# First feed-forward product by one level of Strassen's scheme: seven half-size products in place of eight, the norm factor applied behind the second product

## The chip, the core and the metric

One NeuronCore of a Trainium2 chip. Its engines run their own instruction streams and meet through semaphores: PE (TensorE, matrix products into PSUM), DVE (VectorE) and ACT (ScalarE) for work on tiles, POOL (GpSimd), and SP (SyncE), whose queue issues nearly all transfers from memory here. The metric is device time of one execution in microseconds (us); lower is better. Three runs of the kernel before took 1042.26, 1042.49 and 1043.43 us, median 1042.49.

## What is computed

One layer of a streaming encoder for 512 prompt tokens and 64 sample tokens, which the kernel treats as one stream of T = 576 columns, model width D = 1024. The change touches the last step of the layer:

```
h = h + mem_attn(rmsnorm(h), mem_k, mem_v, w_mem_q, w_mem_o)
hn = rmsnorm(h, ln_ffn)
h = h + square(relu(hn @ w_ff1)) @ w_ff2        # 1024 -> 4096 -> 1024
y = rmsnorm(h, ln_final)
```

All inputs are float32. The kernel gets near float32 accuracy from faster products on a rounded type ("fp32r"): each operand is split into a high part (a cast) and a low part (operand minus high part), and a product is the sum of high x high, high x low and low x high, the low x low term being dropped.

## The kernel before

Activations lie transposed: 128 of the 1024 features on the partitions, eight such blocks, the 576 tokens along the free dimension. `hT` holds h in that form. `project` (L168) computes one output block of 128 features for all tokens: for each of two token ranges (256 and 320 columns, `HALVES`) it takes a PSUM bank from the "pr" group (three banks) and goes over the blocks of the contraction, three partial products for each. In the range of 256 columns the two products with the high part of the weights share one matmul of 512 columns (`high_parts`, L184); in the range of 320 they are two matmuls. A function `evac` given by the caller empties the bank.

`weights` and `split_weights` (L154) bring weights: SP loads a raw tile (three buffers), ACT casts it to the high part at L160, and DVE subtracts at L161 to get the low part.

The stages around the change, in the program's order:

1. Output projection of the memory attention: eight `project` calls with `w_mem_o`, whose `add_residual` (L1085) adds the result to `hT`, multiplies it by the gain `ln_ffn`, splits it into `fx`, and adds up the squares for the norm.
2. `norm_columns` (L1112): five small matmuls sum the squares over partitions, POOL takes the power -1/2 (`rpow`), and `row_broadcast` spreads the factor 1/rms over all partitions into `rB`.
3. `ff1(g)` (L1218), for eight groups of four output blocks: `project` over all eight blocks of the contraction; the evacuation multiplies by `rB` (L1226), squares the positive part (L1227), and splits the result into high and low parts (L200, L201).
4. Second product: group g-1 of the hidden features is the contraction (four blocks) for each of eight output blocks; `add_residual` adds each result to `hT` (L1090, L1092). The loop issues `ff1(g)` ahead of the second product of group g-1.
5. The last group's weights for the second product are kept (`last_weights`, L1238), and the last products run in two token ranges (`last_block`, L1247), so that the final norm and the output of the first range overlap the second.

The tiles come from pools: "sp" (small tiles), "wp" (weights), "up" (six large pairs) and "cp" (constants). The order of instructions on each engine is fixed when the program is built, by a planner that follows the dependencies; some parts are kept in written order.

Of the kernel before, what the change touches and what calls it, by code (L numbers as in the profile page):

```python
# [37 lines left out]
def hybrid_layer_kernel(  # L38
# [30 lines left out]
    wp = ctx.enter_context(tc.tile_pool(name="wp", bufs=2))  # L69
    sp = ctx.enter_context(tc.tile_pool(name="sp", bufs=2))  # L70
    tp = ctx.enter_context(tc.tile_pool(name="tp", bufs=2))
    ps = ctx.enter_context(tc.tile_pool(name="ps", bufs=2, space=PSUM))
    dp = ctx.enter_context(tc.tile_pool(name="dp", bufs=1, space=bass.MemoryType.DRAM))
    BANKS = dict(pr=3, ba=2, g0=1, g1=1, gs=1)
# [14 lines left out]
    SHARED = dict(cb="p0", yv="p1", fs="p0", ko="p0", tm="p1", r="on", acc="p1")  # L89
# [12 lines left out]
    def const(shape, name, dt=F32):  # L102
        return cp.tile(shape, dt, tag=name, name=name)

    def mm(out, lhsT, rhs, start=True, stop=True, pin=False):
        i = nc.tensor.matmul(out, lhsT, rhs, start=start, stop=stop)  # L106
        if pin:
            tc.keep_in_program_order(i)

# [54 lines left out]
    def weights(w, c0, kt=KT):  # L164

        return split_weights(w[:, c0 : c0 + P], [P, kt, P])
# [25 lines left out]
    def add_to(dst, b, more):  # L192
        A.copy(dst, more)  # L193
        V.tensor_tensor(dst, b, dst, ALU.add)  # L194
# [886 lines left out]
        nc.sync.dma_start(hT[i], hd[i])  # L1081

    accs = [None]

    def add_residual(m, last, split=None, g0=None, alone=None):  # L1085


        def evac(b, a0, n, more):
            hm = hT[m // 4][:, m % 4, a0 : a0 + n]
            V.tensor_tensor(hm, hm, b, ALU.add)  # L1090
            if more is not None:
                V.tensor_tensor(hm, hm, more, ALU.add)  # L1092
            if not last:
                return
            if split is not None:
                split_to(split, hm, m, a0, gcol[:, g0 + m : g0 + m + 1])
            if m == 0:
                if a0 == 0:
                    accs[0] = small("acc", [P, T])
                A.activation(accs[0][:, a0 : a0 + n], hm, AF.Square)  # L1100
            else:
                sq = small("zr", [P, 320])[:, :n]
# [104 lines left out]
                A.copy(dh, src)  # L1207
# [10 lines left out]
    def ff1(g):  # L1218
        sx = (pair((4, 1, 5)[g % 3], F32R),)
        for i in range(4):  # L1220
            def evac(b, a0, n, more):
                f = small("fs", [P, 320])[:, :n]
                if more is not None:
                    add_to(f, b, more)
                    b = f
                V.tensor_tensor(f, b, rB[:, a0 : a0 + n], ALU.mult)  # L1226
                V.scalar_tensor_tensor(f, f, 0.0, f, ALU.max, ALU.mult)  # L1227
                split_to(sx, f, i, a0)

            project(  # L1230
                weights(w_ff1[0], (4 * g + i) * P), fx, evac, between=broadcast if g == i == 0 else None
            )
        return sx


    wlast = []

    def last_weights(m):  # L1238
        if m == 0:
            wlast.extend(pair(i, F32R) for i in (3, 2))  # L1240
        hi, lo = (view(u, m // 4, 16, P)[:, 4 * (m % 4) : 4 * (m % 4) + 4] for u in wlast)
        raw = wp.tile([P, 4, P], F32, tag="raw", name=nm("raw"), bufs=3)
        nc.sync.dma_start(raw, w_ff2[0, (NG - 1) * 512 :, m * P : (m + 1) * P].rearrange("(k p) n -> p k n", p=P))
        A.copy(hi, raw)
        V.tensor_tensor(lo, raw, hi.bitcast(F32), ALU.subtract)
# [44 lines left out]
        rpow(r2[:, c], r[:, c])  # L1290
        return r2

    pend = ff1(0)
    for g in range(1, NG):
        nxt = ff1(g)
        for m in range(KT):
            project(
                weights(w_ff2[0, (g - 1) * 512 : g * 512, :], m * P, 4), pend, add_residual(m, False), kt=4
            )
            if g == NG - 1:  # L1300
                last_weights(m)
        pend = nxt


    for m in range(KT):
        last_block(m, pend, *HALVES[0])
# [50 lines left out]
```

## Time and profile before

| | |
|---|---|
| time, median of 3 runs | 1042.49 us (1042.26 to 1043.43) |
| profiled execution: span from first to last instruction | 1039.2 us |
| mean granted TensorE clock | 0.998 |
| busy share: PE, DVE, ACT, POOL | 98%, 65%, 43%, 6% |
| instructions of the span | 16983 |
| output projection of the memory attention | ends near 615 us |
| the two feed-forward products | about 615 to 1030 us |

The profile gives for its execution the span alone; the runs' times also hold what lies around it. Lines of a timeline give start and length in us, engine, line of the kernel, operation, written tile and read tiles, shapes and count; in square brackets stands the idle time before and what ended it. A group's line gives count, then busy us in total and the mean ns of one instruction, then idle time before the group's instructions. A windows line gives the window, its length, and for PE, weight loads (PEld), DVE, ACT and POOL the busy us and the count, then the granted clock, the share of the DMA engines and GB/s. Matmuls overlap: one starts before the one before it has drained, so the time that a matmul costs is the distance between starts.

### The profile page before, as it was taken

To read this page: it belongs to the slowest core of one execution; us is meant where nothing else is said; L and a number is where in the kernel's file an instruction comes from. 1 tells how busy PE (TensorE), PEld (TensorE's weight loads), DVE (VectorE), ACT (ScalarE), POOL (GpSimd) and SP (SyncE) were. 2 spreads that over 40 slices of the span, in tenths; PEclk is the share of its full clock that TensorE was granted. 3 is DMA by queue.
4 is the path that set the end of the run, shared out by engine and by line. 5 is a ranking of instruction groups with operands and counts; after the bars stand their busy time and mean duration, and the time that the engine had idled before them with its cause. 6 is when DMAs were issued, how large, how long until landed. Compare 5 with 4: busy or idle time off the path is not lost.

```text
span 1039.2 us, 16983 instructions
## 1 busy us (share of the span) xinstructions
PE 1019.3 (98%) x6566; PEld 931.0 (90%) x6566; DVE 680.0 (65%) x1502; ACT 445.6 (43%) x936; POOL 58.3 (6%) x124
## 2 busy tenths in 40 slices
PE   9999999999999999999999999999999999999996
PEld 7989899998888878999987999999999999999996
DVE  6676784776666676665664756666666666666763
ACT  6654664433465665444543433323222222222344
POOL 3431110100001000000000000000000000000000
PEclk9999999999999999999999999999999999999999
DMA  7433410100321445433120222141313132313312
GB/s 214 128 102 83 116 50 26 38 21 22 110 83 47 145 164 188 136 84 121 41 62 21 81 82 72 41 122 51 113 51 112 54 110 61 112 52 112 96 48 92
DMA packets 139748, 89.97 MB, mean 87 GB/s; under 512 B 5570, under 2 KB 130624, under 8 KB 139156
## 3 DMA queue, kind: packets, MB, share of 16 engines
q1 hardware_dynamic: 139300, 88.24, 29.0%
q8 instruction: 52, 0.85, 0.3%
q10 hardware_dynamic: 368, 0.66, 0.2%
q14 instruction: 28, 0.23, 0.1%
HBM read 79.14 MB, written 9.74 MB: 86 GB/s over the span
## 4 chain that ended last, share of the span: by engine, by line
PE 87%; DVE 3%; issue 2%; POOL 2%; ACT 2%; DMA 1%; POOLq 0%; ACTq 0%; DVEq 0%; SPq 0%
PE pr L106 68%; PE g L106 9%; PE gs L106 5%; PE ba L112 2%; PE g L112 2%; DVE wl L161 0%; PE ba L106 0%; POOL tg L207 0%; DVE p L456 0%; DMA out_dram<-S 0%; DMA S<-in_state_gdn_dram 0%; POOL tiny L207 0%; POOL X L603 0%; DVE on L779 0%; ACT L644 0%
## 5 line engine op out<-in xcount | busy, mean ns | idle before, releaser
L106 PE MATMUL pr<-u,wh 128*128 128x320 f32 (+2 forms) x2680 | 691.4, 340 | 2.1 <-DVE p L322 1.0
L106 PEld LDWEIGHTS pr<-u,wh 128*128 128x128 f32 x2680 | 456.6, 188 | 36.5 <-DVE p L322 1.3
L106 PE MATMUL pr<-u,wl 128*128 128x256 f32 (+1 forms) x1776 | 482.4, 299 | 0.0
L106 PEld LDWEIGHTS pr<-u,wl 128*128 128x128 f32 x1776 | 327.0, 189 | 7.7 <-issue 0.7
L160 ACT CAST wh<-raw 128x1024 fp32r<-128x1024 f32 (+1 forms) x153 | 136.6, 892 | 223.5 <-PE pr L106 214.9
L161 DVE TENSOR_TENSOR wl<-raw,wh 128x1024 fp32r<-128x1024 f32 (+1 forms) x153 | 157.4, 1029 | 52.9 <-ACT wh L160 50.8
L1090 DVE TENSOR_TENSOR u<-u,pr 128x256 f32<-128x256 f32 (+1 forms) x160 | 72.4, 453 | 61.7 <-PE pr L106 59.1
L200 ACT CAST u<-p 128x256 fp32r<-128x256 f32 x64 | 27.8, 434 | 51.8 <-DVE p L1227 51.8
L207 POOL TENSOR_TENSOR tiny<-tiny,nhalf 128x1 f32<-128x1 f32 (+4 forms) x11 | 10.4, 946 | 645.0 <-DVE tiny L1289 409.0
L106 PE MATMUL pr<-wh,u 128*128 128x512 f32 x128 | 41.2, 400 | 0.0
L201 DVE TENSOR_TENSOR u<-p,u 128x256 fp32r<-128x256 f32 x64 | 29.2, 457 | 15.1 <-ACT u L200 15.1
L193 ACT COPY p<-pr 128x256 f32<-128x256 f32 (+1 forms) x42 | 15.6, 372 | 49.4 <-PE pr L106 49.4
L1092 DVE TENSOR_TENSOR u<-u,pr 128x256 f32<-128x256 f32 x80 | 33.6, 420 | 2.4
L194 DVE TENSOR_TENSOR p<-pr,p 128x256 f32<-128x256 f32 (+1 forms) x42 | 17.8, 423 | 25.8 <-ACT p L193 25.7
L456 DVE SCALAR_TENSOR_TENSOR p<-p,gcol,p 128x579 f32<-128x579 f32 x33 | 27.1, 822 | 9.0 <-ACT p L454 8.5
L1226 DVE TENSOR_TENSOR p<-pr,rB 128x320 f32<-128x320 f32 x32 | 15.7, 492 | 25.6 <-PE pr L106 25.6
L1227 DVE SCALAR_TENSOR_TENSOR p<-p 128x256 f32<-128x256 f32 x64 | 29.3, 458 | 2.2
L203 ACT ACTIVATE u<-u,gcol 128x256 fp32r<-128x256 f32 (+1 forms) x32 | 17.0, 533 | 30.4 <-DVE u L1092 30.4
L106 PE MATMUL g<-u,qz 128*128 128x256 f32 (+4 forms) x96 | 29.2, 408 | 0.0
L741 ACT COPY X<-g 128x512 f32<-128x512 f32 (+1 forms) x24 | 13.2, 551 | 34.3 <-PE g L112 34.3
L106 PEld LDWEIGHTS pr<-wh,u 128*128 128x128 f32 x128 | 23.3, 188 | 4.4
L106 PE MATMUL pr<-u,u 128*128 128x320 f32 (+2 forms) x160 | 26.5, 323 | 0.0
(373 smaller groups left out, 1248.9 us busy)
## 6 DMA issues: line engine op xcount, KB each, us to landing
raw<-in_w_ff_dram SPq DMA_DIRECT2D x32, 512.0 KB
raw<-in_w_ff_dram SPq DMA_DIRECT2D x64, 256.0 KB
raw<-in_w_in_dram SPq DMA_DIRECT2D x28, 512.0 KB
raw<-in_w_mem_k_dram SPq DMA_DIRECT2D x8, 512.0 KB
raw<-in_w_mem_v_dram SPq DMA_DIRECT2D x8, 512.0 KB
raw<-in_w_out_dram SPq DMA_DIRECT2D x8, 512.0 KB
raw<-in_w_mem_q_dram SPq DMA_DIRECT2D x8, 512.0 KB
raw<-in_w_mem_o_dram SPq DMA_DIRECT2D x8, 512.0 KB
```

Of the source, the lines that this page charges most:

```text
L106: i = nc.tensor.matmul(out, lhsT, rhs, start=start, stop=stop)
L112: i = nc.tensor.transpose(out, in_, ident[:n, :n])
L160: A.copy(wh, raw)
L161: V.tensor_tensor(wl, raw, wh.bitcast(F32), ALU.subtract)
L194: V.tensor_tensor(dst, b, dst, ALU.add)
L200: A.copy(h, src)
L201: V.tensor_tensor(lo, src, h.bitcast(F32), ALU.subtract)
L203: A.activation(h, src, AF.Identity, scale=g)
L456: V.scalar_tensor_tensor(yv[:, :n], cb[:, i : i + n], cwt[:, m, i : i + 1], yv[:, :n], ALU.mult, ALU.add)
L1090: V.tensor_tensor(hm, hm, b, ALU.add)
L1092: V.tensor_tensor(hm, hm, more, ALU.add)
L1227: V.scalar_tensor_tensor(f, f, 0.0, f, ALU.max, ALU.mult)
```

## The change

The normalised input is no longer formed. The first product runs on h times the gain, without the factor 1/rms. As relu(c x)^2 = c^2 relu(x)^2 for positive c, the squared factor (a reciprocal on DVE, no root) is multiplied onto the second product's sum, behind the product; only the last group of hidden features gets it ahead of the second product.

`combine(m)` forms, while the output projection runs (in the order m = 0, 4, 1, 5, 2, 6, 3, 7), the combinations of the input's four quarters (upper and lower half of the features, first and second 288 tokens) that the scheme needs, and splits them. `ff1_pair(p)` computes two output blocks: it loads a raw tile of 512 x 256 for each half of the features, forms four sums of weight blocks on DVE, splits seven weight blocks, and runs seven products of 4 x 3 matmuls with 288 columns, accumulating in the banks "g0", "gs", "g1" and "ba"; ACT copies intermediate sums out (`keep`), DVE adds them, squares and splits (`put`). The pools "sp" and "wp" are closed ahead of this, and a new pool "fp" takes tiles in the same memory, waiting tile by tile for the old ones. The second product sums over groups in its own buffer `accu`, which is multiplied by the factor and added to `hT` after group 6. The sum of squares moves into a tile of its own ("accq").

```
@@ output projection, first product @@
-    fx = [pair(i, F32R) for i in (3, 2)]
-    for m in range(KT):
-        project(weights(w_mem_o[0], m * P), mo, add_residual(m, True, fx, G_FF))
-    cols, rB = norm_columns(), const([P, T], "rB")
-    broadcast = lambda: row_broadcast(cols, rB, pin=True)
+    NH = T // 2
+    N0, N1 = slice(0, NH), slice(NH, T)
+    B2 = pair(1, F32R)
+    T12, T34 = ([u[:, j].rearrange("p k (i t) -> p i k t", i=2) for j in range(2)] for u in (pair(2, F32R), pair(3, F32R)))
+    B1 = [cp.tile([P, 2, T], F32R, tag=f"qz{i}", name=nm("B1")).rearrange("p j (k t) -> p j k t", k=2) for i in range(2)]
+    def combine(m):
+        scaled[m] = x = small("kd" if m < 4 else "aT", [P, T])
+        A.activation(x, hT[m // 4][:, m % 4, :], AF.Identity, scale=gcol[:, G_FF + m : G_FF + m + 1])
+        k = m % 4
+        if m < 4:
+            hi, lo = (B1[k // 2][:, j, k % 2, :] for j in range(2))
+            A.copy(hi, x[:, N0])
+            V.tensor_tensor(lo, x[:, N0], hi.bitcast(F32), ALU.subtract)
+            return
+        top = scaled[k]
+        t12, t34 = small("p0", [P, 2, NH]), small("an", [P, 2, NH])
+        V.tensor_tensor(t12[:, 0], top[:, N1], top[:, N0], ALU.subtract)
+        V.tensor_tensor(t34[:, 0], x[:, N1], top[:, N1], ALU.subtract)
+        V.tensor_tensor(t12[:, 1], x[:, N1], t12[:, 0], ALU.subtract)
+        V.tensor_tensor(t34[:, 1], x[:, N0], t12[:, 1], ALU.subtract)
+        for (hi, lo), src in (
+            ((T12[j][:, :, k, :] for j in range(2)), t12),
+            ((B2[:, j, k, :] for j in range(2)), x),
+            ((T34[j][:, :, k, :] for j in range(2)), t34),
+        ):
+            A.copy(hi, src)
+            V.tensor_tensor(lo, src, hi.bitcast(F32), ALU.subtract)
+    for m in (0, 4, 1, 5, 2, 6, 3, 7):
+        project(weights(w_mem_o[0], m * P), mo, add_residual(m, True))
+        combine(m)
...
+    V.tensor_scalar(cols, b[:, :5], 1.0 / D, EPS, ALU.mult, ALU.add)
+    V.reciprocal(squared, cols)
+    work.close()
+    fp = ctx.enter_context(tc.tile_pool(name="fp", bufs=1, reuse_waits="tile"))
+    def split(src, tag, bufs, dma=False):
...
+        with tc.high_priority():
+            A.copy(wh, src)
+            V.tensor_tensor(wl, src, wh.bitcast(F32), ALU.subtract)
+    def weights2(w, c0):
+        raw = ft("r2", [P, 4, P], 3)
+        nc.sync.dma_start(raw, w[:, c0 : c0 + P].rearrange("(k p) n -> p k n", p=P))
+        return split(raw, "w2", 3)
+    def ff1_pair(p, sx):
+        raw = []
+        for i in range(2):
+            raw.append(ft("r1", [P, 4, 2 * P], 2))
...
+        A11, A21 = raw[0][:, :, :P], raw[0][:, :, P:]
+        A12, A22 = raw[1][:, :, :P], raw[1][:, :, P:]
+        s12, s34 = (ft(tag, [P, 2, 4, P], 1) for tag in ("s12", "s34"))
+            V.tensor_tensor(s12[:, 0], A21, A22, ALU.add)
+            V.tensor_tensor(s12[:, 1], s12[:, 0], A11, ALU.subtract)
+        a11, ws12 = split(A11, "a1", 1), split(s12, "w12", 1)
+            V.tensor_tensor(s34[:, 1], A12, s12[:, 1], ALU.subtract)
+            V.tensor_tensor(s34[:, 0], A11, A21, ALU.subtract)
+        a2, ws34 = split(raw[1], "a2", 1), split(s34, "w34", 1)
...
+        def put(i, n, b, more):
+            c = ft("c", [P, NH], 3)
+            V.tensor_tensor(c, b, more, ALU.add)
+            V.scalar_tensor_tensor(c, c, 0.0, c, ALU.max, ALU.mult)
+            if p >= 2 * (NG - 1):
+                V.tensor_tensor(c, c, rB[:, n], ALU.mult)
+            hi, lo = (sx[:, j, 2 * (p % 2) + i, n] for j in range(2))
+            A.copy(hi, c)
+            V.tensor_tensor(lo, c, hi.bitcast(F32), ALU.subtract)
+        x, y, z, w = bank("g0"), bank("gs"), bank("g1"), bank("ba")
+        product(1, x, True)
+        s1 = keep(x)
+        product(5, z, True)
+        s5 = keep(z)
+        product(2, y, True)
+        put(0, N0, y[:, :NH], s1)
+        product(6, x, False)
+        s2 = keep(x)
+        product(3, z, False)
+        put(0, N1, z[:, :NH], s2)
+        product(7, x, False)
+        s3 = keep(x)
+        put(1, N1, s3, s5)
+        product(4, w, True)
+        put(1, N0, w[:, :NH], s3)
@@ the loop over groups @@
-    pend = ff1(0)
+    pend = pair(5, F32R)
+    ff1_pair(0, pend)
+    ff1_pair(1, pend)
+    row_broadcast(squared, rB)
     for g in range(1, NG):
-        nxt = ff1(g)
+        nxt = (f1 if g == 1 else odd()) if g % 2 else pair(5, F32R)
         for m in range(KT):
-            project(
-                weights(w_ff2[0, (g - 1) * 512 : g * 512, :], m * P, 4), pend, add_residual(m, False), kt=4
-            )
+            if m % 4 == 0:
+                ff1_pair(2 * g + m // 4, nxt)
+            project(weights2(w_ff2[0, (g - 1) * 512 : g * 512, :], m * P), (pend,), add_group(g - 1, m), kt=4)
             if g == NG - 1:
-                last_weights(m)
+                am, hm = accu[0][m // 4][:, m % 4, :], hT[m // 4][:, m % 4, :]
+                V.tensor_tensor(am, am, rB, ALU.mult)
+                V.tensor_tensor(hm, hm, am, ALU.add)
+                if m >= 4:
+                    last_weights(2 * m - 8)
+                    last_weights(2 * m - 7)
```

In the built program PE's seven products of a pair stand in the order 1, 5, 2, 6, 3, 7, 4; pairs 0, 1 and 2 follow each other with nothing of the second product between them; from pair 5 on product 1 and most of product 5 are moved between the blocks of the second product.

More of the change, by code (lines that the diff above doesn't have):

```diff
@@ L103, in const, with mm @@
         return cp.tile(shape, dt, tag=name, name=name)
-    def mm(out, lhsT, rhs, start=True, stop=True, pin=False):
-        i = nc.tensor.matmul(out, lhsT, rhs, start=start, stop=stop)
+    def mm(out, lhsT, rhs, start=True, stop=True, pin=False, skip_group_check=False):
+        i = nc.tensor.matmul(out, lhsT, rhs, start=start, stop=stop, skip_group_check=skip_group_check)
         if pin:
@@ L1083, in hybrid_layer_kernel @@
     accs = [None]
+    temps = lambda n: small("zr", [P, 320])[:, :n]
     def add_residual(m, last, split=None, g0=None, alone=None):
@@ new lines, in hybrid_layer_kernel @@
+    for m in (0, 4, 1, 5, 2, 6, 3, 7):
+        project(weights(w_mem_o[0], m * P), mo, add_residual(m, True))
+        combine(m)
+    b = bank()
+    for t, (q0, n) in enumerate(QT):
+        mm(b[:, t : t + 1], accs[0][:, q0 : q0 + n], ones[:, 0:1])
+    cols, squared = tiny([P, 5]), tiny([P, 5])
+    V.tensor_scalar(cols, b[:, :5], 1.0 / D, EPS, ALU.mult, ALU.add)
+    V.reciprocal(squared, cols)
+    work.close()
+    fp = ctx.enter_context(tc.tile_pool(name="fp", bufs=1, reuse_waits="tile"))
@@ new lines, in ft @@
+    def ft(tag, shape, bufs, dt=F32):
+        return fp.tile(shape, dt, tag=tag, name=nm(tag), bufs=bufs)
+    temps = lambda n: ft("tm", [P, 320], 2)[:, :n]
+    odd = lambda: ft("f1", [P, 2, 4, T], 1, F32R)
+    f1 = odd()
+    rB = ft("rB", [P, T], 1)
+    def split(src, tag, bufs, dma=False):
+        shape = list(src.shape)
+        wh, wl = (ft(tag + x, shape, bufs, F32R) for x in "hl")
+        with tc.high_priority():
+            A.copy(wh, src)
+            V.tensor_tensor(wl, src, wh.bitcast(F32), ALU.subtract)
+        return wh, wl
@@ L1236, in hybrid_layer_kernel, with add_group, evac @@
+    accu = [None]
+    def add_group(g, m):
+        def evac(b, a0, n, more):
+            am = accu[0][m // 4][:, m % 4, a0 : a0 + n]
+            if g == 0:
+                if more is not None:
+                    add_to(am, b, more)
+                else:
+                    A.copy(am, b)
+                return
+            V.tensor_tensor(am, am, b, ALU.add)
+            if more is not None:
+                V.tensor_tensor(am, am, more, ALU.add)
+        return evac
     wlast = []
```

61 lines of the change are left out of this document (41 added, 20 removed).

## The prediction

> **What bounds the kernel now.** I read the page's first part, then the windows over the feed-forward stages, then the chain of waits.
>
> ```profile
> PE 1019.3 (98%) x6566; PEld 931.0 (90%) x6566; DVE 680.0 (65%) x1502; ACT 445.6 (43%) x936; POOL 58.3 (6%) x124
> ```
> ```profile
> 760.00:820.00 60.00, 60.00 (x380) 56.49 (x380) 39.03 (x77) 16.45 (x30) 0.00 (x0) 1.00 0.28 80
> 880.00:940.00 60.00, 60.00 (x380) 56.56 (x379) 39.02 (x76) 15.83 (x27) 0.00 (x0) 1.00 0.29 83
> ```
> ```profile
> PE 87%; DVE 3%; issue 2%; POOL 2%; ACT 2%; DMA 1%; POOLq 0%; ACTq 0%; DVEq 0%; SPq 0%
> ```
>
> TensorE (PE) never pauses in the two products: 60.00 of 60.00 us in both windows, granted clock 1.00, and the chain is 87% PE. VectorE (DVE) is busy 39.0 of 60. So a matmul less is worth its start-to-start time, as long as DVE keeps pace. The rhythm stands in PE's timeline:
>
> ```profile
> 701.65 0.40 PE L106 MATMUL pr<-u,wh 128*128 128x512 f32 x1
> 701.89 0.28 PE L106 MATMUL pr<-u,wl 128*128 128x256 f32 x1
> 702.01 0.40 PE L106 MATMUL pr<-u,wh 128*128 128x512 f32 x1
> ...
> 703.07 0.40 PE L106 MATMUL pr<-u,wh 128*128 128x512 f32 x1
> ...
> 704.42 0.31 PE L106 MATMUL pr<-u,wl 128*128 128x320 f32 x1
> ...
> 705.30 0.31 PE L106 MATMUL pr<-u,wl 128*128 128x320 f32 x1
> ```
>
> Four 512+256 pairs take 1.42 us (701.65 to 703.07), so 0.355 a pair, of which the 256 takes 0.12 (701.89 to 702.01). Six of 320 columns take 0.88, so 0.147 each.
>
> **The saving on PE.** An output block of the first product now costs 8 x 0.355 + 24 x 0.147 = 6.36 us, the 32 blocks 203.5. Afterwards a pair of blocks is seven products of 12 matmuls, 84 of 288 columns. No row has 288; halfway between 0.120 and 0.147 lies 0.134, which I take, and the ends are 0.120 and 0.147. Sixteen pairs are 1,344 matmuls, 180.1 us. The saving is **23.4 us** (5.9 to 42 by the ends; the 320 rate costs all but a quarter). The second product keeps its matmuls: 1.42 us for a block's 256 columns, 12 x 0.147 = 1.76 for its 320, 12.7 for four blocks.
>
> **What DVE and ACT get instead.** Durations by form:
>
> ```profile
> L161 DVE TENSOR_TENSOR wl<-raw,wh 128x1024 fp32r<-128x1024 f32 x43 | 52.7, 1225 | 13.5 <-ACT wh L160 11.9
> L160 ACT CAST wh<-raw 128x1024 fp32r<-128x1024 f32 x43 | 45.2, 1050 | 63.2 <-PE pr L106 59.6 <-ACT u L1207 2.1 <-issue 1.4
> L161 DVE TENSOR_TENSOR wl<-raw,wh 128x512 fp32r<-128x512 f32 x56 | 38.6, 690 | 7.0 <-ACT wh L160 6.8
> L1090 DVE TENSOR_TENSOR u<-u,pr 128x320 f32<-128x320 f32 x72 | 35.1, 487 | 46.2 <-PE pr L106 45.7
> L160 ACT CAST wh<-raw 128x512 fp32r<-128x512 f32 x56 | 34.7, 620 | 109.5 <-PE pr L106 106.5 <-DMA raw<-in_w_ff_dram 3.0
> L1092 DVE TENSOR_TENSOR u<-u,pr 128x256 f32<-128x256 f32 x72 | 30.2, 420 | 2.2
> L200 ACT CAST u<-p 128x320 fp32r<-128x320 f32 x32 | 14.8, 462 | 7.1 <-DVE p L1227 7.1
> L200 ACT CAST u<-p 128x256 fp32r<-128x256 f32 x32 | 13.0, 406 | 44.7 <-DVE p L1227 44.7
> ```
>
> Between the rows: 288 columns 0.455 on DVE and 0.43 on ACT; 576 columns 0.757 on DVE and 0.68 on ACT. DVE makes for a pair of blocks four sums of weights and one low part of 512 (5 x 0.69), three low parts of 1024 (3.68), and for each of four outputs an add, a square and a low part (12 x 0.455 = 5.46): 12.6 us. With four blocks of the second product (4 x 0.69 of weights, 4 x (0.42+0.42+0.487) of sums, 8.1) a cycle is 20.7 us of DVE against 84 x 0.134 + 12.7 = 24.0 of PE, 86%. On average it fits. Queued instructions also overlap:
>
> ```profile
> 616.82 1.23 DVE L161 TENSOR_TENSOR wl<-raw,wh 128x1024 fp32r<-128x1024 f32 x1 [0.60 <-ACT wh L160]
> 617.96 0.55 DVE L204 SCALAR_TENSOR_TENSOR u<-u,gcol,u 128x320 fp32r<-128x320 f32 x1
> ```
>
> The second starts 1.14 us after the first, 0.09 before its end; I count 0.08.
>
> **Term 1, the entry.** Today the first weights are asked for at 592.68, some 28 us before the factor's root on POOL:
>
> ```profile
> 592.68 19.41 SPq L156 DMA_DIRECT2D raw<-in_w_ff_dram  x4
> ```
> ```profile
> 620.35 1.17 POOL L207 TENSOR_TENSOR tiny<-tiny,nhalf 128x5 f32<-128x5 f32 x1 [144.26 <-DVE tiny L1117]
> 621.57 1.38 PE L106 MATMUL ba<-ident,tiny 128*128 128x128 f32 x10 [0.81 <-POOL tiny L207]
> ```
>
> The entry's one stall is PE's wait for POOL's root, 0.8 to 1.1 us. That root goes. But the new pool "fp" reuses the memory of "sp", and in the built program SP's first weight load waits for DVE's very last subtraction in `combine(7)`, which reads the tile lying under the load's target. Behind it in SP's queue stand all other weight loads. From PE's last matmul of the output projection, DVE has an add and a sum of squares (2 x 0.487), three combinations (3 x 0.455), three low parts (3 x 0.757) and two tiny ones, 5 us, and waits for ACT's square and scaling, 0.46 + 0.68: about 6.1. Then the load:
>
> ```profile
> 605.38 54.40 SPq L156 DMA_DIRECT2D raw<-in_w_ff_dram  x9
> ```
> ```profile
> 608.50:609.00 0.50, 0.50 (x5) 0.50 (x5) 0.00 (x0) 0.00 (x0) 0.00 (x0) 1.00 0.47 129
> 609.00:609.50 0.50, 0.50 (x5) 0.46 (x4) 0.11 (x1) 0.11 (x1) 0.00 (x0) 1.00 0.00 0
> ```
>
> 512 KB asked for at 605.38 into an idle queue stop flowing just before 609.0: 3.6 us. So raw weights at 9.7, the cast 0.62 later, the first matmul near 10.4, where PE has had 2 us of work. From then DVE is the limit: three pairs run back to back, and ahead of the add that frees the first bank of the second product its queue holds 12 instructions of 1024, 25 of 512, 35 of 288 and two small: 14.7 + 17.3 + 15.9 + 0.7 = 48.6 us, 42.8 with all 72 overlaps. That ends at 52.5 to 58.3. Undelayed PE would be there after 252 x 0.134 + three second-product parts (1.42+1.76+1.42) + 1.7 of small matmuls = 40.1. The lag is 12.4 to 18.2; I take 15.0, as some waits for PE break the overlaps, less the 1.1 that goes: **+13.9**.
>
> **Term 2, the clock.** Eight us without a matmul do not occur today except at the end:
>
> ```profile
> 1031.00:1032.00 1.00, 0.36 (x3) 0.12 (x2) 0.16 (x1) 0.00 (x0) 0.75 (x1) 1.00 0.00 0
> ...
> 1034.00:1035.00 1.00, 0.00 (x0) 0.00 (x0) 0.33 (x1) 0.50 (x1) 0.00 (x0) 0.94 1.02 379
> 1035.00:1036.00 1.00, 0.00 (x0) 0.00 (x0) 0.00 (x0) 0.00 (x0) 0.00 (x0) 0.50 1.03 375
> ```
>
> The granted clock is half some 3.5 us after the last matmul, so the first products start at half speed. How long that lasts no row shows; between nothing and the whole first pair (another 11.3 us, part of it under DVE's work) I take **+1**. [...]
>
> **Term 3, the steady cycles.** The order of the program is tight. Between the end of a pair's seventh product and the point where PE needs the first of its three banks back lie product 4 (1.61), blocks of 1.42 + 1.76 + 1.42 and product 1 of the next pair (1.61): 7.82. DVE's list up to the add that frees it (L1374 in the new file) begins behind 0.4 and 1.05 of ACT casts and holds two low parts of 1024, two instructions of 512, five of 288 and two of 256: 1.45 + 2.45 + 1.38 + 2.28 + 0.84 = 8.4, or 7.6 with ten overlaps. That is 0.2 early, or 0.6 late without overlaps. The second bank is needed after 7.82 + 1.76 + 1.42 + 11 x 0.134 = 12.5. Ahead of its add DVE waits for the next pair's raw weights, whose load SP issues only after the low part of "a2", 4.8 us into the list: 4.8 + 3.6 + five of 512 and two of 256 (4.3, overlapped 3.8) = 12.3, again 0.2 early. There are eleven such cycles. I take 0.1 each, **+1** (0 to 11).
>
> **Term 4, the tail.** The norm factor costs two extra 576-wide instructions for each of eight blocks and one of 288 for each of the last eight outputs, and the last weights (eight of 512) now fall into the last four blocks. From the last product to the third bank of the last blocks DVE's list is 10 x 0.69 + 10 x 0.42 + 7 x 0.757 + 4 x 0.487 + 5 x 0.455 = 20.6, or 17.7 overlapped, where PE has 12.7 + 3 x 1.42 = 17.0. These loads share three buffers with the others:
>
> ```profile
> 979.97 0.37 SPq L1243 DMA_DIRECT2D raw<-in_w_ff_dram  x1
> ```
> ```profile
> 982.95 0.62 ACT L1244 CAST u<-raw 128x512 fp32r<-128x512 f32 x1 [1.53 <-DMA raw<-in_w_ff_dram]
> ```
>
> A load of 256 KB is usable 3.0 us after its issue, and each now waits for the subtraction that frees its buffer; DVE then stands, the adds behind it stand, and PE's banks stay full. 0.7 to 3.6 for the list, up to 3 for the loads, and 0.8 in the cycle before, where two of the factor's 288s lengthen the list of term 3: **+4.5** (1 to 7).
>
> The eight DVE and six ACT instructions of each pair of `combine` calls (four and four today) lie under 2 x 6.36 us of PE, where DVE then has about 11.5; without that cover the eight would cost 5 x 0.455 + 3 x 0.757 = 4.5 us a pair, as the last ones do in term 1.
>
> Sum: -23.4 + 13.9 + 1 + 1 + 4.5 = -3.0. The profiled span is 1039.2 and the runs' median 1042.49, 3.3 us around the span that the change leaves alone: span 1036.2, time **1039.5 us**.
>
> **The rivals.**
> - *A bank short in every cycle* (slower). If the raw load of a cycle lands 4.5 us after its issue, behind others in SP's queue, the second bank is 0.7 late, or 1.4 with the overlaps lost at the waits. At 1.0 eleven cycles cost +11 in place of 1: 1049.5. It decides from 0.4 a cycle on, where the sum turns positive. For it: a margin of 0.2, on an in-order queue. Against: DVE has 3.3 us to spare in a cycle, and an isolated load took 3.6.
> - *The entry costs its bare load only*: PE waits 8 us, and DVE's backlog is hidden: -23.4 + 6.9 + 6.5 = -10.0, 1032.5. Against: the 42.8 us list.
> - *The clock stays low through the first pairs*: +8 in place of 1, 1046.5. For: PE goes on pausing there.
> - *288 columns cost what 320 do*: 1,344 x 0.147 = 197.6, saving 5.9, +14.5, 1057.0. Against: 256 is cheaper than 320 in the rows.
>
> **How the numbers follow.** The sum as worked 0.54 (its own range 1034 to 1045; faster 0.31, no change 0.14, slower 0.09), short banks 0.20, bare load 0.15, low clock 0.07, 320 price 0.04. Faster 0.46, the same 0.14, slower 0.40, where 0.2% (2.1 us) is what a measurement of this kernel can tell from no change. The range 1032 to 1052 reaches the second rival and most of the first, and leaves out the last one and a saving without entry cost.
>
> **What would show it.** After: 1,344 matmuls of 288 columns at 0.134; the first weight load issued some 6 us after the output projection's last matmul and PE idle for about 8 us before the first `g0` product; DVE at 9 tenths for 40 us behind it; a granted clock under 1 there; PE pauses before `pr` matmuls under 0.4 us a cycle, released by L1374; ACT waiting for `r2` loads in the last 40 us. The forecast is wrong if PE is short of 100% in the middle windows (760 to 940 us), or if the gap at the entry is under 4 us.

## The result and the profile after

The changed kernel takes 1038.39 us (median of 5 runs, 1037.32 to 1040.66) against 1042.49 us of the kernel before: ratio 0.9966, 95% interval 0.9953 to 0.9978. The profiled execution spans 1035.6 us where it spanned 1039.2. The forecast was a span of 1036.2 and a time of 1039.5.

The page's first part, each engine's busy time, share of the span and instructions:

```profile
PE 1001.3 (97%) x6630; PEld 921.2 (89%) x6630; DVE 733.2 (71%) x1591; ACT 488.5 (47%) x1024; POOL 56.4 (5%) x123
```

TensorE is busy for 18 us less, and DVE for 53 us more. (The busy time also holds matmuls at half clock and waits too short to show, so it falls by less than the saving worked out below.) The windows of the changed kernel, in the same columns as before, show where TensorE pauses now:

```profile
610.00:620.00 10.00, 7.45 (x49) 6.96 (x47) 5.61 (x14) 4.44 (x9) 0.00 (x0) 0.91 0.00 0
620.00:630.00 10.00, 3.23 (x12) 3.01 (x13) 5.88 (x10) 4.03 (x6) 0.00 (x0) 0.50 0.63 184
630.00:640.00 10.00, 10.00 (x72) 10.00 (x71) 8.21 (x13) 4.61 (x9) 0.00 (x0) 0.91 0.56 163
640.00:650.00 10.00, 8.26 (x60) 7.71 (x59) 9.73 (x19) 5.10 (x11) 0.00 (x0) 1.00 0.41 127
...
760.00:820.00 60.00, 60.00 (x410) 57.67 (x410) 48.30 (x93) 23.33 (x42) 0.00 (x0) 1.00 0.28 84
...
980.00:1000.00 20.00, 16.16 (x98) 14.38 (x98) 18.54 (x37) 6.82 (x13) 0.00 (x0) 1.00 0.31 92
```

The middle is full, as before, with DVE at 48 of 60 us in place of 39. Two stages have holes: the entry (PE 3.23 of 10 us from 620 on, at half clock) and the tail (16.16 of 20 us from 980 on). The view of waits names them; its columns are the total, the number of waits and the longest:

```profile
PE g L107 <- ACT a1h L1270: 8.0, 1, 8.0
PE pr L107 <- ACT w2h L1270: 3.8, 2, 2.8
PE pr L107 <- DVE u L1342: 1.5, 1, 1.5
PE ba L107 <- DVE accq L1110: 1.3, 1, 1.3
```

Before, the same view from 600 us on held one wait, for POOL (0.8 us). The entry, in the timeline:

```profile
615.60 0.45 PE L107 MATMUL pr<-u,wh 128*128 128x320 f32 x2
615.89 0.50 PE L107 MATMUL ba<-ones,accq 128*128 128x1 f32 x4
...
617.66 1.06 PE L107 MATMUL ba<-ones,accq 128*128 128x1 f32 x6 [1.27 <-DVE accq L1110]
...
618.76 0.17 DVE L1252 TENSOR_SCALAR tiny<-ba 128x5 f32<-128x5 f32 x1 [1.15 <-PE ba L107]
...
621.43 0.76 DVE L1243 TENSOR_TENSOR u<-an,u 128x576 fp32r<-128x576 f32 x1
622.27 0.92 SPq L1288 DMA_DIRECT2D r<-in_w_ff_dram  x2
...
626.10 0.62 ACT L1270 CAST a1h<-r 128x512 fp32r<-128x512 f32 x1 [4.70 <-DMA r<-in_w_ff_dram]
626.10 0.69 DVE L1298 TENSOR_TENSOR s<-r 128x512 f32<-128x512 f32 x1 [3.91 <-DMA r<-in_w_ff_dram]
...
626.77 0.85 PE L107 MATMUL g<-B,a1h 128*128 128x288 f32 x2 [8.05 <-ACT a1h L1270]
...
636.04 0.69 DVE L1293 TENSOR_TENSOR s<-r,r 128x512 f32<-128x512 f32 x1 [1.79 <-DMA r<-in_w_ff_dram]
...
641.52 0.46 DVE L1342 TENSOR_TENSOR u<-c,u 128x288 fp32r<-128x288 f32 x1
...
642.03 0.50 PE L107 MATMUL pr<-u,w2h 128*128 128x512 f32 x1 [1.50 <-DVE u L1342]
```

The last product of the output projection ends at 616.05. DVE's subtraction from "an" ends at 622.19, SP issues the first weight load at 622.27, ACT and DVE have the weights at 626.10, and the first product starts at 626.77: the chain of term 1, step by step. The last three lines are the entry's second meeting of PE and DVE: the raw weights of the second pair land (636.04), DVE works on up to the low part of the first output (L1342), and the first matmul of the second product, which reads it, starts at 642.03.

For the comparisons below I cut the kernel at marks that every trace has. The **entry** runs from the DVE instruction that takes the norm's sums (L1252) to the fifth pair's first product, the **ten cycles** from the sixth pair's first product to the last pair's, the **tail** from there to the final norm's first sums. In windows of the changed kernel these are:

```profile
618.76:702.94 84.18, 74.25 (x507) 71.89 (x507) 67.00 (x119) 42.60 (x80) 0.00 (x0) 0.92 0.38 114
718.64:959.48 240.84, 240.40 (x1641) 231.28 (x1640) 189.08 (x363) 88.69 (x160) 0.00 (x0) 1.00 0.29 86
959.48:1010.77 51.29, 47.45 (x305) 44.18 (x304) 44.09 (x96) 18.80 (x39) 0.00 (x0) 1.00 0.18 52
```

| kernel | time, us | ratio to before (95%) | entry | ten cycles | tail |
|---|---|---|---|---|---|
| changed | 1038.39 | 0.9966 (0.9953 to 0.9978) | 84.18 | 240.84 | 51.29 |
| early loads | 1033.61 | 0.9920 (0.9905 to 0.9935) | 80.54 | 240.18 | 51.72 |
| early loads, two pairs | 1032.97 | 0.9919 (0.9904 to 0.9934) | 80.44 | 239.86 | 51.84 |
| warm clock | 1039.59 | 0.9979 (0.9969 to 0.9989) | 86.12 | 240.16 | 51.93 |
| light first pairs | 1036.11 | 0.9944 (0.9928 to 0.9961) | 82.88 | 240.47 | 51.90 |
| light first pairs, warm | 1036.07 | 0.9946 (0.9931 to 0.9961) | 81.94 | 240.81 | 51.93 |
| own buffers in the tail | 1035.32 | 0.9942 (0.9925 to 0.9958) | 84.20 | 241.03 | 48.69 |
| early loads and own buffers | 1030.27 | 0.9890 (0.9875 to 0.9904) | 79.15 | 239.96 | 48.71 |
| the same without the factor | 1028.49 | 0.9880 (0.9862 to 0.9897) | 79.87 | 239.83 | 46.84 |
| product 4 twice | 1060.88 | 1.0187 (1.0172 to 1.0202) | 90.52 | 254.55 | other order |
| light later pairs | 1036.66 | 0.9953 (0.9938 to 0.9968) | 85.29 | 238.81 | other order |
| more DVE in later pairs | 1043.14 | 1.0016 (1.0007 to 1.0025) | 85.27 | 242.39 | 53.69 |
| sums of weights on GpSimd | 1045.29 | 1.0034 (1.0022 to 1.0047) | 85.12 | 250.94 | 48.74 |

Times are medians, stages are from one profiled execution each, in us. Each ratio is to runs of the kernel before that were made beside it (medians 1041.29 to 1042.49), so small differences between kernels are better read from the ratios and the stages than from the medians. Where a kernel leaves a stage unchanged, the ten cycles lie between 239.83 and 241.03 and the tail between 51.29 and 51.93; the entry repeats less well (below). The five tails of 51.72 to 51.93 us hold a stretch of 3.4 us at half clock (984.3 to 987.7 us with early loads), the changed kernel's tail holds none. "Other order" means that the planner moved matmuls from the tail ahead of its mark; in the last four kernels it also ordered the cycles anew.

### The profile page after: what moved, and what is told of

It is laid out like the page before. It is cut to its first block, busy times and chain, and to the rows that moved or that the text cites. A ratio compares the mean times of both kernels' runs of the same rounds, so it can differ in the third digit from the quotient of the medians.

```text
span 1035.6 us, 17242 instructions
## 1 busy us (share of the span) xinstructions
PE 1001.3 (97%) x6630; PEld 921.2 (89%) x6630; DVE 733.2 (71%) x1591; ACT 488.5 (47%) x1024; POOL 56.4 (5%) x123
## 4 chain that ended last, share of the span: by engine, by line
PE 79%; DVE 6%; issue 3%; DMA 3%; ACT 3%; POOL 2%; POOLq 0%; ACTq 0%; SPq 0%; DVEq 0%
PE pr L107 46%; PE g L107 19%; PE gs L107 7%; DMA r<-in_w_ff_dram 3%; PE ba L113 2%; PE ba L107 2%; PE g L113 2%; DVE wl L162 0%; ACT w12h L1270 0%; DMA out_dram<-S 0%; POOL tg L208 0%; DVE p L457 0%; DVE a2l L1271 0%; DVE c L1336 0%; DVE c L1337 0%
## 5 line engine op out<-in xcount | busy, mean ns | idle before, releaser
L107 PE MATMUL pr<-u,wh 128*128 128x320 f32 (+2 forms) x1240 | 328.5, 342 | 1.8 <-DVE p L323 1.0
L107 PE MATMUL pr<-u,wl 128*128 128x256 f32 (+1 forms) x816 | 228.1, 303 | 0.0
L107 PEld LDWEIGHTS pr<-u,wh 128*128 128x128 f32 x1240 | 211.6, 188 | 18.1 <-DVE p L323 1.3
L107 PEld LDWEIGHTS pr<-u,wl 128*128 128x128 f32 x816 | 149.4, 188 | 3.8 <-issue 0.7
L162 DVE TENSOR_TENSOR wl<-raw,wh 128x1024 fp32r<-128x1024 f32 x65 | 79.5, 1224 | 36.6 <-ACT wh L161 36.1
L107 PE MATMUL pr<-u,w2h 128*128 128x320 f32 (+1 forms) x384 | 98.7, 340 | 5.5 <-ACT w2h L1270 3.8
L161 ACT CAST wh<-raw 128x1024 fp32r<-128x1024 f32 x65 | 68.2, 1049 | 60.5 <-PE pr L107 54.8
L107 PE MATMUL pr<-f,w2h 128*128 128x320 f32 (+1 forms) x288 | 74.7, 340 | 0.3 <-DVE u L1374 0.2
L107 PEld LDWEIGHTS pr<-u,w2h 128*128 128x128 f32 x384 | 64.9, 188 | 10.9 <-ACT w2h L1270 4.4
L107 PE MATMUL pr<-u,w2l 128*128 128x256 f32 (+1 forms) x256 | 65.2, 295 | 0.0
L107 PEld LDWEIGHTS pr<-f,w2h 128*128 128x128 f32 x288 | 48.6, 188 | 4.1 <-issue 1.3
```

Of the source, the lines that this page charges most:

```text
L107: i = nc.tensor.matmul(out, lhsT, rhs, start=start, stop=stop, skip_group_check=skip_group_check)
L161: A.copy(wh, raw)
L162: V.tensor_tensor(wl, raw, wh.bitcast(F32), ALU.subtract)
```

## The experiments

**1. First weights where nothing is late.** s12 and s34 are asked for ahead of r1, so r1's buffers move up by 8 KB, onto memory that comes free sooner: SP issues the first weight loads at 587.64 here, where it issued them at 622.27. The order of PE's matmuls in the first four pairs stays the same.

```diff
+        s12, s34 = (ft(tag, [P, 2, 4, P], 1) for tag in ("s12", "s34"))
         raw = []
         for i in range(2):
             raw.append(ft("r1", [P, 4, 2 * P], 2))
...
-        s12, s34 = (ft(tag, [P, 2, 4, P], 1) for tag in ("s12", "s34"))
```

> The changed kernel with the request for s12 and s34 ahead of the one for r1, so that the first weights no longer lie on the memory of combine's last tile. If DVE's list behind the entry sets the lag, as forecast: the list starts at DVE's last subtraction of combine (622.2) and not when the load lands (626.1), the order on DVE being the same, so 3.9 us less, about 1034.5. If PE's own gap is what is lost: the first product follows the last cast of combine plus one cast (622.0 instead of 626.8), 4.7 us less, 1033.7. If the load was not what held the entry: no change, 1038.

1033.61 us, and the entry is 3.6 us shorter. The timeline of this kernel (DVE's last subtraction, PE's first product, DVE's first sum of weights, and the second meeting):

```profile
621.70 0.76 DVE L1243 TENSOR_TENSOR u<-an,u 128x576 fp32r<-128x576 f32 x1
...
622.24 0.85 PE L107 MATMUL g<-B,a1h 128*128 128x288 f32 x2 [3.25 <-ACT a1h L1270]
622.37 0.68 DVE L1298 TENSOR_TENSOR s<-r 128x512 f32<-128x512 f32 x1
...
632.45 0.69 DVE L1293 TENSOR_TENSOR s<-r,r 128x512 f32<-128x512 f32 x1 [2.25 <-DMA r<-in_w_ff_dram]
...
638.44 0.50 PE L107 MATMUL pr<-u,w2h 128*128 128x512 f32 x1 [1.08 <-DVE u L1342]
```

DVE goes from its last subtraction straight into the sums, at 622.37 and not 626.10, 3.7 us sooner. PE's gap is 3.25 in place of 8.05 us, 4.8 less, and the stage gains 3.6. That the load's place in memory held the entry is shown. The second meeting tells the two sizes apart: the second pair's raw weights land 3.6 us sooner (632.45 for 636.04), PE waits for L1342 in both kernels, and its matmul there starts 5.99 us after that landing in both. So the entry gains what DVE's chain gains, and the rest of PE's shorter gap is lost again at this wait.

**2. A clock that doesn't drop.** Sixty matmuls into a bank that nothing reads fill the gap.

```diff
     V.reciprocal(squared, cols)
+    b = bank()
+    for i in range(60):
+        mm(b[:, :NH], B1[i % 2][:, 0, 0, :P], B1[i % 2][:, 0, 1], pin=True)
     work.close()
```

> The changed kernel with 60 extra matmuls of 288 columns (8.0 us at full clock) behind the norm's sums, into a bank that nothing reads, so that TensorE does not fall idle at the entry. If the half clock of the first 5 us (2.5 us) is lost time: 1035.9. If DVE's list sets the lag, as forecast, PE only waits 2.5 us longer for the first bank of the second product: no more than 0.5 us, 1038, with a new wait of about 2 us before a pr matmul near 670 us.

No gain: 1039.59 us, with a ratio whose interval overlaps the changed kernel's, and the entry is 1.9 us longer. The waits of this kernel from 618 to 700 us (L1345 is L1342 of the changed kernel, three lines lower):

```profile
PE pr L107 <- DVE u L1345: 3.2, 1, 3.2
PE ba L107 <- DVE accq L1110: 1.3, 1, 1.3
```

The 8-us gap is gone, the first products run at full clock, and what PE wins there it waits out in front of the first `pr` product: 3.2 us in place of 1.5, for the low part that DVE makes. This matmul starts 5.99 us after the second pair's raw weights landed (642.93 after 636.94), as it does at half clock (642.03 after 636.04). So the half clock after the gap costs nothing here of its own. That the entry came out longer has two visible causes: the second pair's raw weights landed later (DVE waited 2.6 us for them, 1.8 in the changed kernel), and the clock dropped all the same, behind that new wait:

```profile
640.00:641.00 1.00, 0.00 (x0) 0.00 (x0) 1.00 (x4) 0.87 (x1) 0.00 (x0) 1.00 0.18 49
...
643.00:644.00 1.00, 0.76 (x3) 0.44 (x4) 1.00 (x2) 1.00 (x2) 0.00 (x0) 1.00 0.18 60
644.00:645.00 1.00, 1.00 (x7) 1.00 (x7) 1.00 (x2) 0.03 (x1) 0.00 (x0) 0.67 0.00 0
646.00:647.00 1.00, 1.00 (x6) 1.00 (x5) 0.52 (x2) 0.00 (x0) 0.00 (x0) 0.50 0.49 88
```

**3. Less DVE at the entry.** In the first three pairs no low part of the weights is made.

```diff
-        a11, ws12 = split(A11, "a1", 1), split(s12, "w12", 1)
+        low = not (p < 3)
+        a11, ws12 = split(A11, "a1", 1, low), split(s12, "w12", 1, low)
...
-        a2, ws34 = split(raw[1], "a2", 1), split(s34, "w34", 1)
+        a2, ws34 = split(raw[1], "a2", 1, low), split(s34, "w34", 1, low)
```

In `split`, `if low:` stands ahead of the subtraction, and `wh` is returned in place of `wl` where it is false, so that PE has as many matmuls as before; the planner put them in another order. The second kernel adds the sixty matmuls of experiment 2.

> The changed kernel without the low part of the weights in the first three pairs: DVE's subtractions behind those splits (three times 0.69 and three of 1.22 us, 13 us) are left out and the matmuls read the high part a second time, so PE's work is the same. If DVE's list behind the entry sets the lag: PE's later waits there (1.9 us) and some small ones (0.9) go, up to 2.8 us less, about 1036; the gap of 8 us stays, as the load still comes late. If the lag is the gap, the clock and late loads alone: no change, 1038.

> The same with the 60 extra matmuls in the gap. If the half clock costs only where DVE's list doesn't hold PE back: now it shows, 2.5 us below the run without them (about 1033.5). If the second pair's late load holds PE in any case: no better than without them.

1036.11 us, the entry 1.3 us shorter: the 1.5-us wait for L1342 is gone and the 8-us gap stays (8.2 us). With the clock kept up as well, the time is the same, 1036.07, and the entry another 0.9 us shorter, not 2.5. So DVE's list did hold PE by that 1.5 us. What took up the rest of the full clock's gain in the second kernel is the sixty matmuls themselves. Its trace:

```profile
620.40 9.82 PE L107 MATMUL ba<-B 128*128 128x288 f32 x60
...
627.96 0.62 ACT L1273 CAST a1h<-r 128x512 fp32r<-128x512 f32 x1 [4.74 <-DMA r<-in_w_ff_dram]
...
630.05 1.76 PE L107 MATMUL g<-B,a1h 128*128 128x288 f32 x12
```

Here the clock fell at 620.2, just ahead of the sixty matmuls, and stayed at half until 623.6; they took 9.82 us where they took 8.23 in experiment 2, and PE came to the first product at 630.05, 1.5 us after its weights were cast (628.58). From the first product on, the entry is 2.3 us shorter than without them (72.5 against 74.8), near the 2.5 expected. So with DVE lightened the half clock does seem to cost PE time, as far as one execution of each shows, with PE's order differing between the two.

**4. The second pair's raw weights, too.** For the second pair `raw[i]` is cut from the memory that accu gets later (`spare[:, i]`, 1024 elements of a partition), and the loads of the first two pairs keep the program's order.

> The early loads, and the second pair's raw weights loaded into the memory of accu (free from 616 to 668), so that they don't wait for the r1 buffers of the first pair. In the run with early loads DVE still waits 3.7 us for raw weights. If DVE's list sets the lag, these go: 2 to 3.7 us below that run (1033.6), about 1031. If PE's own sequence is the limit by now: no more than 0.5 us below it.

1032.97 us, 0.6 below the run with early loads, with the same ratio (0.9919 against 0.9920); the entry is 80.44 against 80.54. DVE's waits for raw weights are shorter (3.7 us with early loads; here 0.9), yet nothing is gained. The forecast's picture, in which the list's length alone sets the lag, fails here: with the loads early, the list is no longer the only bound. The planner ordered PE's matmuls anew, the wait for L1342 is gone, and PE waits for DVE 0.7 and 0.6 us at two other places. The half clock is then no longer covered by a wait: it lasts 7.2 us from the first product on, some 3.6 us of PE's time by an estimate at half speed, from the granted clock of 0.50.

Experiment 6 has the same PE order in its entry as experiment 1, and its entry is 1.4 us shorter (79.15 against 80.54). Its clock also stays at half for less: 4.9 us from the first product on (622.60 to 627.5), 7.1 in experiment 1 (622.24 to 629.3). Windows of experiment 1's kernel, then of experiment 6's:

```profile
628.00:629.00 1.00, 1.00 (x6) 1.00 (x6) 1.00 (x3) 0.45 (x3) 0.00 (x0) 0.50 0.54 109
629.00:630.00 1.00, 1.00 (x8) 1.00 (x8) 1.00 (x2) 0.52 (x1) 0.00 (x0) 0.84 0.90 277
```
```profile
627.00:628.00 1.00, 1.00 (x8) 1.00 (x7) 1.00 (x3) 1.00 (x2) 0.00 (x0) 0.74 0.97 328
628.00:629.00 1.00, 1.00 (x9) 1.00 (x9) 1.00 (x2) 0.72 (x2) 0.00 (x0) 1.00 0.62 185
```

The clock is not the cause of that difference, though: PE waits for L1342 in both (1.1 and 1.0 us). The second pair's raw weights, asked for 6.0 us after the norm's sums in both, landed 13.4 us after them in experiment 1 and 12.3 in experiment 6. In the changed kernel and in experiments 1, 2, 5, 6 and 7, the first matmul of the second product starts 5.99 or 6.00 us after that landing. The entry ends 66.8 to 67.1 us after it in all of them but experiment 2 (68.2), where the second stretch of half clock lies in between. So in these kernels the second pair's raw weights set the entry's length, through DVE's list behind them. Why the same loads took 1.1 us longer in one execution is not shown.

**5. Own buffers in the tail.** The last weights are loaded two blocks at a time into r1's buffers.

```diff
     def last_weights(m):
...
-        raw = ft("r2", [P, 4, P], 3)
-        nc.sync.dma_start(raw, w_ff2[0, (NG - 1) * 512 :, m * P : (m + 1) * P].rearrange("(k p) n -> p k n", p=P))
-        A.copy(hi, raw)
-        V.tensor_tensor(lo, raw, hi.bitcast(F32), ALU.subtract)
+        raw = ft("r1", [P, 4, 2 * P], 2)
+        nc.sync.dma_start(raw, w_ff2[0, (NG - 1) * 512 :, m * P : (m + 2) * P].rearrange("(k p) n -> p k n", p=P))
+        for i in range(2):
+            hi, lo = (view(u, m // 4, 16, P)[:, 4 * (m % 4 + i) : 4 * (m % 4 + i) + 4] for u in wlast)
+            A.copy(hi, raw[:, :, i * P : (i + 1) * P])
+            V.tensor_tensor(lo, raw[:, :, i * P : (i + 1) * P], hi.bitcast(F32), ALU.subtract)
...
                     last_weights(2 * m - 8)
-                    last_weights(2 * m - 7)
```

> The changed kernel with the last weights loaded two blocks at a time into the buffers of r1, free by then, in place of the three r2 buffers. If the shared buffers hold the tail: PE's two waits for w2h there (2.8 and 1.0 us) go, 3.8 us less, about 1034.6. If DVE's list (17.7 to 20.6 us against 17.0 of PE) holds it: at most 0.5 us less, 1038, with the waits now released by DVE.

1035.32 us, the tail 2.6 us shorter. The waits of this kernel from 960 to 1010 us:

```profile
PE pr L107 <- DVE u L1094: 0.9, 1, 0.9
PE pr L107 <- DVE u L1372: 0.3, 2, 0.2
```

The 3.8 us of waiting for `w2h` are gone, and 1.2 us of waiting for DVE have come in their place: both parts of the forecast's term are real, and the loads were the larger.

**6. Both edits.**

> Both edits, the early loads and the tail's own buffers: the two stages are 300 us apart, so the gains add, 3.9 + 3.8 = 7.7 us less, about 1030.7; 1033 to 1034 if one of them is nothing.

1030.27 us, 8.1 us below the changed kernel. This version beats both kernels: 0.9890 of the time before (0.9875 to 0.9904).

**7. The factor in the tail.** Experiment 6 without `V.tensor_tensor(am, am, rB, ALU.mult)` and without the multiplication by `rB` in `put`.

> The kernel with early loads and the tail's own buffers, with the norm factor left out: no multiplication of accu (eight of 576 columns) and none in the last group's puts (eight of 288), so the output lacks the factor in its second feed-forward term. In the run with the factor DVE works without a pause from 972.4 to 993.5 us there, and PE waits 1.3 us for it. If the factor's instructions (8 x 0.67 + 8 x 0.37 = 8.3 us of DVE) are what makes DVE late in the tail: the 1.3 us go, about 1029.0 against 1030.3. If DVE catches up anyway, or the remaining waits are for the weights: no change, 1030.3.

1028.49 us, the tail 1.9 us shorter. (The ratios, 0.9880 and 0.9890, differ by 1.0 us, with overlapping intervals; the entry of this execution was 0.7 us longer.) The tail in windows, of experiment 6 and of this kernel:

```profile
954.19:1002.90 48.71, 47.48 (x305) 44.11 (x304) 43.62 (x96) 18.27 (x39) 0.00 (x0) 1.00 0.13 41
```
```profile
954.96:1001.80 46.84, 46.84 (x305) 44.13 (x304) 36.86 (x82) 18.80 (x39) 0.00 (x0) 1.00 0.13 40
```

PE is busy for all of its 46.84 us. So the changed kernel's tail of 51.29 us holds 4.45 us that PE doesn't need: 2.6 by the shared buffers, 1.9 by the factor's work on DVE.

**8. What a product is worth.**

```diff
         product(4, w, True)
+        product(4, w, True)
         put(1, N0, w[:, :NH], s3)
```

> The changed kernel with product 4 run twice in each pair (its bank is started anew, so the sum is the same): 192 matmuls of 288 columns more, the number that a plain product of this size would have. If PE is the bound in all sixteen pairs: 192 x 0.1327 = 25.5 us more, 1063.9. If DVE holds the first three pairs: these hide up to 4.8 us of it, and the small waits of the later cycles another 2: 18.7 us more, 1057.

1060.88 us, 22.5 us above the changed kernel. The entry's four pairs pay their four products in full (6.3 us, by 4 x 12 x 0.133 = 6.4), so DVE hides nothing there, in an order that the planner made anew. The ten cycles pay 13.7 of 16.0. A cycle is 25.5 us, by 96 x 0.133 + 12.7 = 25.5: the small waits of the changed kernel's cycles, 0.2 us each, are gone.

**9. The cycles: less DVE.** The condition of experiment 3 turned round, `low = not (p >= 3)`.

> The changed kernel without the low part of the weights from the fourth pair on (DVE's subtractions left out, the high part read a second time): 4.35 us of DVE less in each of thirteen pairs. The ten cycles from 714 to 955 us took 240.8 us, where 84 x 0.1327 and four blocks of 3.17 make 238.3. If these 2.5 us are waits for DVE: they go, about 1036, and nothing more, as PE is the bound. If they are costs of PE itself: no change, 1038.

1036.66 us. The ten cycles in a window:

```profile
727.41:966.22 238.81, 238.81 (x1643) 230.81 (x1642) 152.03 (x324) 92.01 (x160) 0.00 (x0) 1.00 0.28 84
```

PE has no pause and takes 238.81 us: so the 2.0 us more in the changed kernel's ten cycles (1.0 to 2.2 in the other kernels that leave the cycles alone) were small waits and not a cost of PE itself. That they were waits for DVE is likely, but this run alone does not show it: the one that the changed kernel's view lists there is released by DVE (L1374, 0.2 us), but with less DVE work the planner also kept a pair's products together on PE.

**10. The cycles: more DVE.**

```diff
             V.tensor_tensor(c, b, more, ALU.add)
+            if p >= 3:
+                V.tensor_tensor(c, c, c, ALU.max)
```

> The changed kernel with one more DVE instruction of 288 columns (the maximum of c with itself, which changes nothing) in each put from the fourth pair on: 52 of them, 0.37 to 0.46 us each, 19 to 24 us of DVE. If the margin of 0.2 us to the banks is real, as the forecast counted: the list gets 0.7 us longer up to the first bank and 1.5 up to the second, so 0.5 to 1.3 us in each of some twelve cycles, 6 to 15 us more, 1044 to 1053, with PE waits before pr released by DVE. If DVE's idle time of 3 us in a cycle takes it up: at most 1 us more.

1043.14 us, 4.8 us more, but the ten cycles grow by 1.6 us only, 0.16 each; the rest is in the tail (2.4), which here holds 6.8 us at half clock (992.1 to 999.0), and at the entry, with the fourth pair (1.1). PE's waits for the line that frees the banks (L1374, here L1376) grow from 0.2 us to 2.2 in eight places, at most 0.5 each. DVE's idle time takes up the rest: the planner, which ordered the program anew, found places for it. A bank short by 1 us in every cycle, the forecast's first rival, doesn't come of 1.5 us more work.

**11. The sums on GpSimd.** In experiment 6's kernel the four sums of a pair run on GpSimd from the fourth pair on (`E = V if p < 3 else G`).

> The kernel with early loads and the tail's own buffers, with the four sums of weights of each pair from the fourth on moved from DVE to GpSimd, which idles there. If the cycles' small waits are DVE's and GpSimd makes four sums of 512 columns well within a cycle of 24 us: 2 to 2.5 us below the run without (1030.3), about 1028. If GpSimd's sums come late or disturb DVE: no gain, or 1 us a cycle more, 1040.

1045.29 us, 15 us more than experiment 6; a cycle is 25.1 us in place of 24.0, and the entry, which ends with the fourth pair, is 6.0 us longer. The timeline of one cycle:

```profile
766.43 1.44 POOL L1299 TENSOR_TENSOR s<-r 128x512 f32<-128x512 f32 x1 [14.38 <-DVE w34l L1271]
766.63 2.32 DVE L1271 TENSOR_TENSOR a2l<-r,a2h 128x1024 fp32r<-128x1024 f32 x1
...
771.88 0.53 PE L107 MATMUL pr<-u,w2h 128*128 128x320 f32 x2 [1.05 <-DVE u L1375]
```

The subtraction for `a2l` takes 2.32 us here, and 2.31 or 2.32 in thirteen of the sixteen pairs, where all sixteen take 1.21 or 1.22 in experiment 6. It starts 0.2 us after GpSimd's sum, which then has 1.24 of its 1.44 us left, and takes 1.10 us longer. The delay comes out at PE in full, as a wait of 1.05 us before a bank that L1375 (L1374 in the changed kernel) frees; there are ten waits of the kind, 10.5 us in all. The subtraction ends 1.08 us after that sum (768.95 against 767.87), and the 1.10 us are within 0.14 of what the sum had left, as if it stood nearly still until then; what holds it up is not shown. The run answers experiment 10 from the other side: here a delay of 1.1 us inside an instruction is paid almost whole, which fits the margin of about 0.2 us that the forecast counted. That the planner could not place work around this delay, as it did in experiment 10, is an explanation and not shown.

## Why the forecast held, point by point

**The saving.** Foreseen 23.4 us at 0.134 us a matmul. Twelve matmuls of one product in the changed kernel:

```profile
760.62 0.43 PE L107 MATMUL ba<-u,a2h 128*128 128x288 f32 x2
...
762.22 0.40 PE L107 MATMUL pr<-u,w2h 128*128 128x512 f32 x1
```

1.60 us, 0.133 each: 1,344 are 179.2, the saving 24.3. Experiment 8 shows that PE pays such a matmul. The price of 320 columns is out.

**Term 1, the entry.** Load 6.2 us after the last product (foreseen 6.1), usable 3.8 later (3.6), first product 10.7 after the last one (10.4), gap 8.05 (8). DVE's list from the first sum to the first evacuation of a bank ran from 626.10 to 672.17, 46.1 us, or 43.3 without its 2.8 us of waits for loads and ACT (foreseen 42.8 to 48.6). The lag with the clock in it: from the first small matmul behind the last product (615.89) to the fifth pair 87.0 us; four pairs (44.7), eight blocks of the second product (25.3) and small matmuls (2.2) make 72.2; so 14.8, less the old 1.1, 13.7, where terms 1 and 2 were 14.9.

The size was right, but the place was not, so the size was partly luck. The forecast let DVE be late at the add that frees the first bank of the second product. That add ran at 672.17, and the view of PE's waits has none for it (L195): behind 643 us it holds only one wait of the entry, 0.2 us for ACT. From start to start, the 14.8 us are 1.4 for the sums of squares, 8.3 for the gap, 2.5 for 5.0 us at half clock (an estimate from the granted 0.50), 1.7 for L1342 at 642.03 and some 0.9 of small waits. DVE's list does set the lag, but through its first 16 us, up to L1342, and with the second pair's raw weights in the middle of them (experiments 1 and 4). The forecast saw neither.

**Term 2, the clock.** This step was wrong in kind. The forecast added 1 us for the half clock on top of the list, a choice between its two ends that no run shows. The granted clock did fall, to 0.50, and stayed there until 5.0 us after the first product; but experiment 2 takes it away and gains nothing, since PE then waits for DVE. A cost on PE seems to count only where PE is the one that is late, as the two kernels of experiment 3 suggest (72.5 against 74.8 us from the first product on). The size of the term is small enough to hide in term 1's.

**Term 3, the cycles.** Foreseen 0.1 us each; 0.2 measured (240.84 against 238.81 in experiment 9), probably for DVE, as foreseen. The rival of 1.0 a cycle did not come, though experiment 11 shows that one delayed instruction is enough to bring it on.

**Term 4, the tail.** Foreseen 4.5 us; 4.45 measured, 2.6 for the loads and 1.9 for the factor. The forecast gave the list 0.7 to 3.6 and the loads up to 3.

With the measured terms: -24.3 + 13.7 + 2.0 + 4.5 = -4.1. The output projection ends 0.35 us later (615.89 against 615.54), which leaves -3.8; the spans differ by 3.6. That the forecast of the time came within 1.1 us is in part luck too: the saving was 0.9 us larger, the cycles cost 1.0 us more, and term 1 had its size from another place than foreseen.

Of the signs listed ahead, one failed: PE's pauses in the middle are not released by L1374 in rows of the waits view (one of 0.2 us is), since most are below what it lists. They show only in the length of the cycle. The middle windows are full or within 0.2 us of it, and the gap is over 4 us.

The rivals: the bare load alone (1032.5) falls, as the entry's lag is 13.7 and not 6.9; the low clock (1046.5) falls, as the clock was back 5.0 us after the first product, and with experiment 2.

## What to carry to other kernels

When a stage's memory is handed to the next, look at which old tile lies under the *first* thing that the new stage loads, and who reads it last: here one reordered request was worth 4.8 us of the time (3.6 in the entry's one profile), as much as the whole change. A saving on the bound engine was paid out in the steady part here and largely given back at the two ends, where PE waited for loads and for DVE; count the ends separately. Ask too whether the engine that loses time is the late one at the next meeting point: with the clock kept up in experiment 2, PE waited there 3.2 us in place of 1.5, and nothing was gained (a ratio of 0.9979 against 0.9966).

## What was not expected of the hardware

The clock's drop came with a delay after a pause, and in experiment 2 it fell into work that had begun again: PE paused from 639.75 to 642.93, and the half clock ran from 644.3 to 647.8, when PE was busy. In the changed kernel it fell from 1.00 to 0.50 at 618.1, 2.05 us after the last product, with eight matmuls of one column in between. In the eleven kernels in which it fell ahead of the first product and was still low there, it came back 4.7 to 7.2 us after that product. The stretches at half clock lasted 13.65 us in the changed kernel (618.10 to 631.75), 10.24 in experiment 1 (619.07 to 629.31), 6.82 in experiment 6 (620.69 to 627.51) and 3.41 in experiment 2: four, three, two and one times 3.41 us. Why the lengths come in such steps, and what sets the delay of the drop, is not shown.
